# Attention scores from stacked high and low parts of queries and keys, in a two-layer network on one core

## The chip, the cores and the metric

The kernel runs on one core of one Trainium2 chip. The metric is the device time of one execution in microseconds (us). The core has TensorE for matrix products (PE in the profile, its weight loads PEld), VectorE (DVE), ScalarE (ACT), GpSimd (POOL) and the sync engine (SP), which here only issues transfers.

## The reference, cut to what matters

Two layers on 512 tokens of width 1024. Layer one mixes a convolution and a recurrence, layer two is attention in a sliding window of 128 with 16 query heads on 4 key heads of 64, and each is followed by a feed-forward part with a gate. The change is in the attention:

```python
q = partial_rope(rms_norm(q, q_norm_g), positions)
k = partial_rope(rms_norm(k, k_norm_g), positions)
...
s = jnp.einsum('bnqhgd,bnkhd->bnhgqk', q, kc).astype(jnp.float32) * (HEAD_DIM ** -0.5)
...
m = jnp.maximum(jnp.max(s, axis=-1, keepdims=True), sink)
pr = jnp.exp(s - m)
pr = pr / (jnp.sum(pr, axis=-1, keepdims=True) + jnp.exp(sink - m))
o = jnp.einsum('bnhgqk,bnkhd->bnqhgd', pr.astype(vc.dtype), vc)
```

Queries come in blocks of 128 tokens; each block sees its own 128 keys and the 128 before them.

## The kernel before, in words

Large products (`gemm`) run on parts: weights and activations are each split into a high part of type fp32r (a copy on ScalarE, line 150 or 183) and a low part (the difference on VectorE, line 151 or 184), and three fp32r products high·high, high·low and low·high are summed in PSUM (line 174). Weights come through SP's queue, 512 KB a transfer, into two buffers (`wraw`, line 139).

`attention` first makes the keys (two gemm blocks of 128 channels), normalises and rotates them (`rope`), and copies each key head by GpSimd's queue (line 867) into both halves of the rows of a tile `kd[m]`, so that either half of the rows can be the contraction. Then come the values (line 876, fp32r products with 256 moving columns), then eight `queries(j)`, each a gemm of 128 channels, two heads. In `rope` for queries, four small transfers on GpSimd's queue (line 835) swap the rotated rows into `zr`. The result lies in `qr[:, j, :]` in fp32, an even head in rows 0 to 63 and an odd one in rows 64 to 127. The queries' norm is not applied to `qr` but kept as a factor `rq` per token and head (lines 902 to 910).

`block(m, b)` treats key head `m` with its four query heads for token block `b`. It makes four fp32 products of 64 rows (line 931) into two PSUM banks `pscs`, one for even and one for odd heads; then, for each head, a VectorE instruction with mask, factor and running minimum (line 936) and an exponential on ScalarE (line 939, shown under the helper's line 101); sums and a reciprocal `dn`; four scalings by `dn` on VectorE (line 946); transposes on TensorE (950), copies on ScalarE (952), products with the values (957), and the split of the output (line 959). For `b = 0` there are 128 keys, otherwise 256. After all blocks the output projection follows, a gemm on `oh` and `ol`.

The calls are written in the order queries 0 and 1, then for each `m` four blocks with one more query ahead of blocks 0 and 2. A planner orders each engine's instructions when the program is built, by written order and by when it reckons that operands and buffers are ready, so that products of later queries stand between those of a block. On the chip each engine works in that fixed order. The scores' PSUM ring `c` has three banks, `a` and `b` have two, `d` has one; the temporary ring `t2` has five tiles.

Of the kernel before, what the change touches and what calls it, by code (L numbers as in the profile page):

```python
# [11 lines left out]
F32 = mybir.dt.float32  # L12
F32R = mybir.dt.float32r
I32 = mybir.dt.int32
AF = mybir.ActivationFunctionType
ALU = mybir.AluOpType
# [3 lines left out]
P = 128  # L20
T = 512
D = 1024
DC = D // P
NB = T // P
# [12 lines left out]
NKV = 4  # L37
HD = 64
# [7 lines left out]
T3 = 5  # L46
# [22 lines left out]
class Net:  # L69
# [734 lines left out]
    def attention(self):  # L804
        nc, tc, ap = self.nc, self.tc, self.ap
        V, S, G = nc.vector, nc.scalar, nc.gpsimd
# [8 lines left out]
        with ExitStack() as es:  # L815
            pool = lambda **k: es.enter_context(tc.tile_pool(**k))
            cst = pool(name="atb", bufs=1)
            tr = pool(name="att", bufs=3)
            t2 = lambda n: tr.tile([P, T], F32, tag="t2", name=n, bufs=T3)
# [3 lines left out]
                G.memset(z, 0.0)  # L823

            def rope(dst, z, j=None):
                t = tq("rp")
                if j is None:
                    pp = self.bank("d")
                    nc.tensor.matmul(pp, lhsT=self.perm, rhs=z, start=True, stop=True)
                    V.tensor_tensor(out=t, in0=pp, in1=sin, op=ALU.mult)  # L830
                else:
                    pp = zr[j % 2]
                    for o in (0, 8, HD, HD + 8):
                        i = o ^ 8
                        G.dma_start(pp[o : o + 8, :], z[i : i + 8, :])
                    V.tensor_tensor(out=t, in0=pp, in1=self.sgs, op=ALU.mult)
                V.tensor_tensor(out=dst, in0=z, in1=cos, op=ALU.mult)
                V.tensor_tensor(out=dst, in0=dst, in1=t, op=ALU.add)


            kd = [cst.tile([P, T], F32, name=f"kd{m}") for m in range(NKV)]
            pk = self.gemm(wq, 8, xh, xl)
            self.table("natural_log_exp_and_others")
            rstd = cst.tile([P, T], F32, name="rstd")
# [8 lines left out]
            for i in range(2):  # L853
                t = tq("zt")
                V.tensor_tensor(out=t, in0=pk[i], in1=rstd, op=ALU.mult)
                S.activation(out=t, in_=t, func=AF.Identity, bias=self.pc("attn_b_qkv", 8 + i))
                sq = tq("zs")
                S.activation(out=sq, in_=t, func=AF.Square)
                pss = self.bank("d")
                nc.tensor.matmul(pss, lhsT=self.bdv, rhs=sq, start=True, stop=True)  # L860
                rs = self.rsqrt_rows(tr, "t2", pss, 1e-6, "kr", ln=True)
                V.scalar_tensor_tensor(out=t, in0=t, scalar=self.pc("attn_k_norm_g"), in1=rs, op0=ALU.mult, op1=ALU.mult)
                kr = tq("kr")
                rope(kr, t)
                for e in range(2):
                    for o in range(2):
                        G.dma_start(kd[2 * i + e][o * HD : (o + 1) * HD, :], kr[e * HD : (e + 1) * HD, :])

            vt = cst.tile([P, NB, KD], F32, name="vt")
            pvs = [self.pmm() for _ in range(NB)]  # L870
# [10 lines left out]
                V.scalar_tensor_tensor(out=vt[:, b, :], in0=pvs[b][:, :KD], scalar=rt[:, b : b + 1], in1=self.bvr, op0=ALU.mult, op1=ALU.add)  # L881


            qr = cst.tile([P, 8, T], F32, name="qr")
            rq = cst.tile([P, NB, NH], F32, name="rq")

            def queries(j):
# [2 lines left out]
                V.tensor_tensor(out=t, in0=pq, in1=rstd, op=ALU.mult)  # L890
                sq = tq("zs")
                S.activation(out=sq, in_=t, func=AF.Square, bias=self.pc("attn_b_qkv", j))
                pss = self.bank("d")[:, 0:8].rearrange("p (b h) -> p b h", b=NB)

                for b in range(NB):
                    for i in range(0, P, 32):
                        nc.tensor.matmul(pss[i : i + 32, b, :], lhsT=sq[:, b * P + i : b * P + i + 32], rhs=self.bh, start=True, stop=True,
                                         tile_position=(0, i))
                S.activation(out=t, in_=t, func=AF.Identity, scale=self.pc("attn_q_norm_g"), bias=self.bg[:, j : j + 1])

                ms = tr.tile([P, NB, 2], F32, tag="ms", name="ms")
                V.tensor_scalar(out=ms, in0=pss, scalar1=1.0 / HD, scalar2=1e-6, op0=ALU.mult, op1=ALU.add)
                rope(qr[:, j, :], t, j)
                y0 = tr.tile([P, NB, 2], F32, tag="my", name="my")
                self.fn(out=y0, in_=ms, func=AF.Ln)
                self.fn(out=y0, in_=y0, func=AF.Exp, scale=-0.5)
                V.tensor_tensor(out=ms, in0=ms, in1=y0, op=ALU.mult)
                V.tensor_tensor(out=ms, in0=ms, in1=y0, op=ALU.mult)
                V.tensor_scalar(out=ms, in0=ms, scalar1=0.5 / 8, scalar2=-1.5 / 8, op0=ALU.mult, op1=ALU.add)
                V.tensor_tensor(out=rq[:, :, 2 * j : 2 * j + 2], in0=ms, in1=y0, op=ALU.mult)  # L910

            cst.tile([P, 112], F32, name="gap")
            oh = cst.tile([P, DC, T], F32R, name="oh")
            ol = cst.tile([P, DC, T], F32R, name="ol")

            def block(m, b):
# [8 lines left out]

                pscs = [self.bank("c").rearrange("p (g k) -> p g k", g=2) for _ in range(2)]
                for hp in range(2):
                    for e in range(2):
                        h = 4 * m + 2 * hp + e
                        hs = slice(e * HD, (e + 1) * HD)  # L930
                        nc.tensor.matmul(pscs[e][:, hp, :nk], lhsT=qr[hs, h // 2, bs], rhs=kd[m][hs, k0 : k0 + nk], start=True, stop=True)  # L931
                for hp in range(2):
                    for e in range(2):
                        i = 2 * hp + e
# [8 lines left out]
                V.tensor_tensor(out=dn, in0=dn, in1=nm, op=ALU.add)  # L943
                V.reciprocal(out=dn, in_=dn)
                for i in range(4):
                    V.tensor_scalar(out=pr_[:, i, :nk], in0=pr_[:, i, :nk], scalar1=dn[:, i : i + 1], scalar2=None, op0=ALU.mult)
                for kb in range(nkb):
                    pt = self.bank("b").rearrange("p (h q) -> p h q", h=4)
                    for i in range(4):
# [95 lines left out]
```

## Time and profile before

| | us |
|---|---|
| median of 3 runs (lowest to highest) | 1216.67 (1216.54 to 1217.11) |
| profiled execution | 1216.95 |
| its span, first to last instruction | 1215.2 |
| TensorE busy | 1194.8 |
| VectorE busy | 723.4 |
| ScalarE busy | 554.3 |
| GpSimd busy | 72.0 |

Times within the span count from its start. The attention's queries, scores and output lie between 695 and 815 us. An instruction's duration includes its latency, and instructions of one engine may overlap in the records; what one costs in a row of its kind is seen in the distance of their starts. An fp32 product stands in the trace as two records, an fp32r product as one.

### The profile page before, as it was taken

To read this page: it belongs to the slowest core of one execution; us is meant where nothing else is said; L and a number is where in the kernel's file an instruction comes from. 1 tells how busy PE (TensorE), PEld (TensorE's weight loads), DVE (VectorE), ACT (ScalarE), POOL (GpSimd) and SP (SyncE) were. 2 spreads that over 40 slices of the span, in tenths; PEclk is the share of its full clock that TensorE was granted. 3 is DMA by queue.
4 is the path that set the end of the run, shared out by engine and by line. 5 is a ranking of instruction groups with operands and counts; after the bars stand their busy time and mean duration, and the time that the engine had idled before them with its cause. 6 is when DMAs were issued, how large, how long until landed. Compare 5 with 4: busy or idle time off the path is not lost.

```text
span 1215.2 us, 16956 instructions
## 1 busy us (share of the span) xinstructions
PE 1194.8 (98%) x6419; PEld 940.5 (77%) x6419; DVE 723.4 (60%) x1366; ACT 554.3 (46%) x1035; POOL 72.0 (6%) x209
## 2 busy tenths in 40 slices
PE   6999999999999999999999999999999999999998
PEld 5777866568788888888888866668888888888886
DVE  6787866477766555553333778875555555553332
ACT  6878332374534444342222567764543343442221
POOL 4101031000100000000000031100000000000000
PEclk9999998999999999999999999999999999999999
DMA  6144291023322223233333231112222223233331
GB/s 191 37 130 113 96 221 38 2 88 103 97 92 104 94 97 104 87 104 96 96 96 95 87 95 57 41 36 90 101 90 101 103 89 104 88 103 112 113 113 61
DMA packets 65088, 114.43 MB, mean 94 GB/s; under 512 B 15680, under 2 KB 17936, under 8 KB 65008
## 3 DMA queue, kind: packets, MB, share of 16 engines
q1 hardware_dynamic: 60048, 102.25, 26.3%
q0 software_dynamic: 4816, 10.89, 3.5%
q8 instruction: 50, 0.82, 0.3%
q14 instruction: 30, 0.25, 0.1%
q10 hardware_dynamic: 144, 0.23, 0.1%
HBM read 105.40 MB, written 4.26 MB: 90 GB/s over the span
## 4 chain that ended last, share of the span: by engine, by line
PE 94%; DVE 2%; ACT 2%; DMA 1%; issue 1%; SPq 0%; DVEq 0%
PE mm L174 68%; PE bank L174 11%; PE mm L633 2%; PE bank L931 2%; PE bank L957 1%; PE bank L950 1%; PE ps L411 1%; PE ps L543 1%; DMA xT<-in_xT_dram 1%; PE ps L562 1%; PE ps L556 1%; PE ps L570 0%; PE bank L359 0%; PE ps L549 0%; PE ps L520 0%
## 5 line engine op out<-in xcount | busy, mean ns | idle before, releaser
L151 DVE TENSOR_TENSOR wlo<-wraw,whi 128x512 fp32r<-128x512 f32 x364 | 250.8, 690 | 348.0 <-ACT whi L150 347.4
L150 ACT CAST whi<-wraw 128x512 fp32r<-128x512 f32 x364 | 224.9, 619 | 421.3 <-PE mm L174 378.4
L174 PE MATMUL mm<-xgh,whi 128*128 128x512 f32 x896 | 350.9, 392 | 9.8 <-ACT whi L150 8.3
L174 PE MATMUL mm<-xgh,wlo 128*128 128x512 f32 x896 | 351.0, 392 | 0.2 <-DVE wlo L151 0.2
L174 PE MATMUL mm<-xgl,whi 128*128 128x512 f32 x896 | 350.5, 391 | 0.0
L174 PEld LDWEIGHTS mm<-xgh,whi 128*128 128x128 f32 x896 | 168.6, 188 | 47.0 <-ACT whi L150 10.1
L174 PEld LDWEIGHTS mm<-xgh,wlo 128*128 128x128 f32 x896 | 168.5, 188 | 38.7 <-issue 2.4
L174 PEld LDWEIGHTS mm<-xgl,whi 128*128 128x128 f32 x896 | 168.7, 188 | 35.8 <-issue 1.2
L174 PE MATMUL mm<-hh,whi 128*128 128x512 f32 x352 | 136.9, 389 | 0.0
L174 PE MATMUL mm<-hl,whi 128*128 128x512 f32 x352 | 136.9, 389 | 0.0
L174 PE MATMUL mm<-hh,wlo 128*128 128x512 f32 x352 | 136.9, 389 | 0.0
L174 PEld LDWEIGHTS mm<-hh,wlo 128*128 128x128 f32 x352 | 66.1, 188 | 13.8
L174 PEld LDWEIGHTS mm<-hh,whi 128*128 128x128 f32 x352 | 66.1, 188 | 13.8
L174 PEld LDWEIGHTS mm<-hl,whi 128*128 128x128 f32 x352 | 66.1, 188 | 13.5
L720 DVE SCALAR_TENSOR_TENSOR t<-gp,col,t 128x512 f32<-128x512 f32 x88 | 63.5, 745 | 0.0
L717 ACT ACTIVATE t<-gp,col 128x512 f32<-128x512 f32 x44 | 35.7, 816 | 35.3 <-DVE gp L715 34.7
L183 ACT CAST hh<-t 128x512 fp32r<-128x512 f32 x44 | 27.2, 622 | 36.8 <-DVE t L723 36.5
L715 DVE TENSOR_TENSOR gp<-mm,rstd 128x512 f32<-128x512 f32 x44 | 30.3, 692 | 17.3 <-PE mm L174 17.2
L723 DVE TENSOR_TENSOR t<-t,mm 128x512 f32<-128x512 f32 x44 | 30.1, 687 | 17.0 <-PE mm L174 17.0
L101 ACT ACTIVATE t<-t 128x512 f32<-128x512 f32 x44 | 27.7, 630 | 20.4 <-DVE t L720 20.3
L714 POOL MEMSET gp<- 128x2 f32 x44 | 4.5, 104 | 507.7 <-DVE t L720 451.0
L936 DVE CUSTOM_DVE_ANT_0 pr<-bank,mask,nsnk 128x256 f32<-128x256 f32 (+1 forms) x64 | 31.4, 503 | 1.9 <-PE bank L931 1.9
(328 smaller groups left out, 1433.6 us busy)
## 6 DMA issues: line engine op xcount, KB each, us to landing
wraw<-in_w_up_dram SPq DMA_DIRECT2D x88, 512.0 KB, 3.5
wraw<-in_w_down_dram SPq DMA_DIRECT2D x40, 512.0 KB, 3.5
wraw<-in_w_in_dram SPq DMA_DIRECT2D x22, 512.0 KB, 3.6
wraw<-in_w_qkv_dram SPq DMA_DIRECT2D x12, 512.0 KB, 3.5
wraw<-in_w_out_dram SPq DMA_DIRECT2D x8, 512.0 KB, 3.5
wraw<-in_w_o_dram SPq DMA_DIRECT2D x8, 512.0 KB, 3.5
st<-cpad POOLq DMA_DIRECT2D x24, 135.0 KB, 4.4
xT<-in_xT_dram SPq DMA_DIRECT2D x4, 512.0 KB, 8.2
```

The lines of the kernel that those rows point to most:

```text
L101: ins = self.nc.scalar.activation(**kw)
L150: nc.scalar.copy(hi, src)
L151: nc.vector.tensor_tensor(out=lo, in0=src, in1=hi.bitcast(F32), op=ALU.subtract)
L174: mm = lambda a, b, **kw: self.nc.tensor.matmul(ps, lhsT=a[:, i, k, :], rhs=b[:, kk, :], **kw)
L183: nc.scalar.copy(hi, src)
L633: nc.tensor.matmul(pc[b * 32 : b * 32 + 32, :], lhsT=dg[:, b, g, :], rhs=stk[b][:, 4 * g : 4 * g + T], start=g == 0, stop=g == 7, tile_pos ...
L715: V.tensor_tensor(out=gp[:, 2:], in0=pg[i], in1=rstd, op=ALU.mult)
L717: S.activation(out=t, in_=gp[:, 2:], func=AF.Identity, scale=self.pc("ffn_conv_w", (3 * l + 2) * FC + f), bias=self.pc("ffn_conv_b", l * F ...
L720: V.scalar_tensor_tensor(out=t, in0=gp[:, j : j + T], scalar=self.pc("ffn_conv_w", (3 * l + j) * FC + f), in1=t, op0=ALU.mult, op1=ALU.add)
L723: V.tensor_tensor(out=t, in0=t, in1=pu[i], op=ALU.mult)
L931: nc.tensor.matmul(pscs[e][:, hp, :nk], lhsT=qr[hs, h // 2, bs], rhs=kd[m][hs, k0 : k0 + nk], start=True, stop=True)
L936: V.tensor_tensor_reduce(out=pr_[:, i, :nk], in0=pscs[e][:, hp, :nk], in1=mask[:, 2 * P - nk :], op0=ALU.add, op1=ALU.min, scale=rq[:, b, ...
```

## The change

The keys are split into a high and a low part after the rotation (`ks`), and both parts are copied into `kd[m]`, now fp32r with two parts. The rotated queries, too, are split, and four transfers a query on SP's queue (`nc.sync`) lay the parts into `qs[m]`: for each pair of heads a tile of 128 rows that holds one head's high part in one half of the rows and its low part in the other. A score is then two products of 128 rows: the stacked query parts by the keys' high part (which stands in both halves) and by the keys' low part, summed in PSUM. They always take 256 keys. `qs` and `ks` share a ring of two tiles. The norm factors of the queries are worked out for two queries at once. Of the four scalings by `dn`, two go to GpSimd. The rotation's temporary moves from a ring of its own to `t2`, and two unused gaps in memory are resized.

```diff
             def rope(dst, z, j=None):
-                t = tq("rp")
+                t = t2("rp")
...
-            kd = [cst.tile([P, T], F32, name=f"kd{m}") for m in range(NKV)]
+            cst.tile([P, 56], F32, name="gap0")
+            kd = [cst.tile([P, 2, T], F32R, name=f"kd{m}") for m in range(NKV)]
+            pair = lambda n: tr.tile([P, 2, 2, T], F32R, tag="qs", name=n, bufs=2)
+            ks = pair("ks")
...
-                kr = tq("kr")
+                kr = t2("kr")
                 rope(kr, t)
+                self.split(ks[:, i, 0, :], ks[:, i, 1, :], kr)
                 for e in range(2):
                     for o in range(2):
-                        G.dma_start(kd[2 * i + e][o * HD : (o + 1) * HD, :], kr[e * HD : (e + 1) * HD, :])
+                        G.dma_start(kd[2 * i + e][o * HD : (o + 1) * HD].bitcast(F32), ks[e * HD : (e + 1) * HD, i].bitcast(F32))
...
-            qr = cst.tile([P, 8, T], F32, name="qr")
+            qs = {}
...
-                pss = self.bank("d")[:, 0:8].rearrange("p (b h) -> p b h", b=NB)
+                if j % 2 == 0:
+                    qs["ps"] = self.bank("d")[:, 0:16].rearrange("p (b i h) -> p b i h", b=NB, i=2)
+                pss = qs["ps"][:, :, j % 2]
...
-                ms = tr.tile([P, NB, 2], F32, tag="ms", name="ms")
-                V.tensor_scalar(out=ms, in0=pss, scalar1=1.0 / HD, scalar2=1e-6, op0=ALU.mult, op1=ALU.add)
-                rope(qr[:, j, :], t, j)
-                y0 = tr.tile([P, NB, 2], F32, tag="my", name="my")
...
+                qr = t2("qr")
+                rope(qr, t, j)
+
+                if j % 2 == 0:
+                    qs[j // 2] = pair("qs")
+                q = [tr.tile([P, T], F32R, tag="t2", name=n, bufs=T3) for n in ("qh", "ql")]
+                self.split(q[0], q[1], qr)
+                for e in range(2):
+                    for d in range(2):
+                        nc.sync.dma_start(qs[j // 2][d * HD : (d + 1) * HD, j % 2, e, :].bitcast(F32), q[d ^ e][e * HD : (e + 1) * HD, :].bitcast(F32))
+                if j % 2:
+
+                    ms = tr.tile([P, NB, 4], F32, tag="ms", name="ms")
+                    V.tensor_scalar(out=ms, in0=qs["ps"].rearrange("p b i h -> p b (i h)"), scalar1=1.0 / HD, scalar2=1e-6, op0=ALU.mult, op1=ALU.add)
+                    y0 = tr.tile([P, NB, 4], F32, tag="my", name="my")
...
+                    V.tensor_tensor(out=rq[:, :, 2 * j - 2 : 2 * j + 2], in0=ms, in1=y0, op=ALU.mult)
+
+            cst.tile([P, 56], F32, name="gap")
...
                 for hp in range(2):
-                    for e in range(2):
-                        h = 4 * m + 2 * hp + e
-                        hs = slice(e * HD, (e + 1) * HD)
-                        nc.tensor.matmul(pscs[e][:, hp, :nk], lhsT=qr[hs, h // 2, bs], rhs=kd[m][hs, k0 : k0 + nk], start=True, stop=True)
+                    for j in range(2):
+                        for e in range(2):
+                            nc.tensor.matmul(pscs[e][:, hp, :], lhsT=qs[m][:, hp, e, bs], rhs=kd[m][:, j, k0 : k0 + 2 * P], start=j == 0, stop=j == 1)
...
                 for i in range(4):
-                    V.tensor_scalar(out=pr_[:, i, :nk], in0=pr_[:, i, :nk], scalar1=dn[:, i : i + 1], scalar2=None, op0=ALU.mult)
+                    (G if i % 2 else V).tensor_scalar(out=pr_[:, i, :nk], in0=pr_[:, i, :nk], scalar1=dn[:, i : i + 1], scalar2=None, op0=ALU.mult)
```

## Rows read from the trace of the kernel before

**Rows 1.** The page: busy times, and the chain that ended last.

```profile
PE 1194.8 (98%) x6419; PEld 940.5 (77%) x6419; DVE 723.4 (60%) x1366; ACT 554.3 (46%) x1035; POOL 72.0 (6%) x209
...
PE 94%; DVE 2%; ACT 2%; DMA 1%; issue 1%; SPq 0%; DVEq 0%
```

**Rows 2.** Stretch: length, busy PE, PEld, DVE, ACT, POOL, clock, DMA.

```profile
715.00:815.00 100.00, 98.79 (x703) 62.64 (x702) 83.20 (x326) 74.09 (x227) 12.22 (x26) 1.00 0.14 42
```

**Rows 3.** Stretch, line 931 alone: length, PE, PEld, clock, DMA.

```profile
715.00:805.00 90.00, 26.55 (x128) 15.19 (x128) 1.00 0.15 47
```

**Rows 4.** Timeline of PE at the first blocks: start us, us, what.

```profile
719.18 0.92 PE L931 MATMUL bank<-kd,qr 64*128 64x128 f32 x6
...
720.83 0.40 PE L174 MATMUL bank<-xgl,whi 128*128 128x512 f32 x1
721.06 0.39 PE L174 MATMUL bank<-xgh,wlo 128*128 128x512 f32 x1
721.38 1.13 PE L931 MATMUL bank<-kd,qr 64*128 64x256 f32 x4
722.44 0.50 PE L174 MATMUL bank<-xgh,whi 128*128 128x512 f32 x1
722.77 0.40 PE L174 MATMUL bank<-xgl,whi 128*128 128x512 f32 x1
...
724.72 1.13 PE L931 MATMUL bank<-kd,qr 64*128 64x256 f32 x8
726.37 0.53 PE L950 MATMUL bank<-ident,pr 128*128 128x128 f32 x2 [0.52 <-DVE pr L946]
```

**Rows 5.** Waits of PEld, 715 to 805: us in total, times, longest.

```profile
PEld bank L931 <- issue: 4.1, 13, 0.4
```

**Rows 6.** Timeline of PE at the values' products.

```profile
681.46 0.28 PE L876 MATMUL mm<-whi,xgh 128*128 128x256 f32 x1
...
681.81 0.28 PE L876 MATMUL mm<-whi,xgh 128*128 128x256 f32 x1
```

**Rows 7.** ACT by shape, 715 to 815: count, busy, mean ns, idle before.

```profile
L150 ACT CAST whi<-wraw 128x512 fp32r<-128x512 f32 x14 | 8.7, 619 | 5.7 <-PE bank L174 5.7
```

**Rows 8.** Timeline of DVE, at the masks and at the first blocks.

```profile
312.42 0.88 DVE L219 TENSOR_TENSOR sq<-sq 128x512 f32<-128x512 f32 x1
313.22 0.88 DVE L151 TENSOR_TENSOR wlo<-wraw,whi 128x512 fp32r<-128x512 f32 x1
...
717.97 0.69 DVE L838 TENSOR_TENSOR qr<-qr,rp 128x512 f32<-128x512 f32 x1
...
725.44 0.68 DVE L838 TENSOR_TENSOR qr<-qr,rp 128x512 f32<-128x512 f32 x1
726.04 0.87 DVE L946 TENSOR_SCALAR pr<-pr,dn 128x128 f32<-128x128 f32 x4
...
728.82 0.87 DVE L946 TENSOR_SCALAR pr<-pr,dn 128x256 f32<-128x256 f32 x3
```

**Rows 9.** Timeline of POOL, at the masks and the keys' copies.

```profile
312.28 0.47 POOL L795 TENSOR_SCALAR_AFFINE_SELECT mask<-mask 128x256 f32<-128x256 f32 x1
...
313.01 0.55 POOL L796 TENSOR_SCALAR_AFFINE_SELECT mask<-mask 128x256 f32<-128x256 f32 x1
...
706.51 2.11 POOL L867 DMA_DIRECT2D kd<-kr  x4
```

**Rows 10.** DMA issues, 695 to 815: KB each, median us to landing.

```profile
wraw<-in_w_o_dram SPq DMA_DIRECT2D x5, 512.0 KB, 3.5
kd<-kr POOLq DMA_DIRECT2D x8, 128.0 KB, 2.8
```

**Rows 11.** DVE by shape, 715 to 815: count, busy, mean ns, idle before.

```profile
L946 DVE TENSOR_SCALAR pr<-pr,dn 128x256 f32<-128x256 f32 x48 | 13.9, 347 | 0.1
...
L184 DVE TENSOR_TENSOR ol<-bank,oh 128x256 fp32r<-128x256 f32 x15 | 6.4, 424 | 5.0 <-ACT oh L183 4.9
...
L946 DVE TENSOR_SCALAR pr<-pr,dn 128x128 f32<-128x128 f32 x16 | 3.6, 280 | 0.0
...
L908 DVE TENSOR_TENSOR ms<-ms,my 128x8 f32<-128x8 f32 x6 | 1.0, 160 | 0.0
```

**Rows 12.** Waits of SP's queue, 715 to 815: us in total, times, longest.

```profile
SPq L139 <- DVE wlo L151: 97.1, 7, 23.9
```

More of the change, by code (lines that the diff above doesn't have):

```diff
@@ L899, in queries @@
                 S.activation(out=t, in_=t, func=AF.Identity, scale=self.pc("attn_q_norm_g"), bias=self.bg[:, j : j + 1])
-                ms = tr.tile([P, NB, 2], F32, tag="ms", name="ms")
-                V.tensor_scalar(out=ms, in0=pss, scalar1=1.0 / HD, scalar2=1e-6, op0=ALU.mult, op1=ALU.add)
-                rope(qr[:, j, :], t, j)
-                y0 = tr.tile([P, NB, 2], F32, tag="my", name="my")
[L905 to L912, printed above, removed]
+                qr = t2("qr")
[11 more added lines that the diff above has]
+                    y0 = tr.tile([P, NB, 4], F32, tag="my", name="my")
+                    self.fn(out=y0, in_=ms, func=AF.Ln)
+                    self.fn(out=y0, in_=y0, func=AF.Exp, scale=-0.5)
+                    V.tensor_tensor(out=ms, in0=ms, in1=y0, op=ALU.mult)
+                    V.tensor_tensor(out=ms, in0=ms, in1=y0, op=ALU.mult)
+                    V.tensor_scalar(out=ms, in0=ms, scalar1=0.5 / 8, scalar2=-1.5 / 8, op0=ALU.mult, op1=ALU.add)
+                    V.tensor_tensor(out=rq[:, :, 2 * j - 2 : 2 * j + 2], in0=ms, in1=y0, op=ALU.mult)
+            cst.tile([P, 56], F32, name="gap")
             oh = cst.tile([P, DC, T], F32R, name="oh")
```

## The prediction

> **What bounds the kernel now.** I read the page's busy times first: TensorE is busy 98% of the span, every other engine 60% or less, and the chain that ended last is TensorE for 94% [rows 1]. That is an average, so I went to the stage of the change. The table by stretches shows 715 to 815 us, nearly the whole attention: TensorE busy 98.79 of 100 us at granted clock 1.00 (the 2.4 GHz level), VectorE 83.2, ScalarE 74.1, GpSimd 12.2 [rows 2]. The reader is to see two things: a microsecond of TensorE work that goes is a microsecond of time here, and VectorE and ScalarE have only some 17 and 26 us of slack behind it.
>
> **Scores, the work removed.** Restricted to the score line, the stretches show TensorE busy 26.55 us in 715 to 805 with 128 records [rows 3]. There are 64 products (16 blocks of 4 heads); each fp32 product is two records. In order of time, four records of 64x256 (two products) start at 721.38 and the next product follows at 722.44, so a product alone costs 0.53 us. At 724.72 eight records take the same 1.13 us, since there the even and odd heads, which lie on different 64 rows, run side by side [rows 4]. The mean (26.55/64 = 0.41) says that both happen. Before a group there is also a gap: the weight product at 721.06 starts 0.32 us before the score, where its neighbours follow in 0.23 [rows 4]. The waits show 13 such entries with no other cause [rows 5]; 13 x 0.09 = 1.2 us, which I count only at the favourable end, since entries from fp32 transposes stay.
>
> **Scores, the work added.** Each block now issues 2 head pairs x 2 key parts x 2 heads = 8 products, 128 rows by 128 columns with 256 moving columns, also in the first block of each group (128 columns before). 16 x 8 = 128. The trace has this very shape: the products of the values at line 876 are fp32r, 128*128, 128x256, and stand 0.12 us apart, each with its own weight load [rows 6]. 128 x 0.12 = 15.4 us. Net 15.4 - 26.55 = **-11.2 us**. Bounds: -12.4 with the entry gaps; -8.6 if 26 groups (twice the 13 entries, an estimate) still show 0.10 us each at their start, as weight products do after a score (0.33 from 722.44 to 722.77, with 0.23 as the pace) [rows 4].
>
> **Query parts and their way to the matmul.** Eight times: a ScalarE cast (0.62, by the weights' cast of the same 128x512) [rows 7], a VectorE subtraction and four transfers of 128 KB on SP's queue. VectorE's instructions overlap in the records: the 128x512 one at 725.44 lasts 0.68, and the next starts 0.60 later [rows 8], so I price by spacing. The second query's rotation ends at 718.66 [rows 8], and scores from it follow from 719.18 [rows 4]. Now they wait 0.62 + 0.69 + 0.53 (issue, as the keys' copies take it, four in 2.11 [rows 9]) + 2.8 (landing of these copies of the same 128 KB [rows 10]) = 4.6 us more. The cover is weight products of queries 2 and 3. It ends: in the trace TensorE already idles 0.52 us at 726.37, at the first transposes, with those products used up [rows 4]. Query 4's products (24 x 0.23 = 5.5 us) could be pulled ahead, if its weights are there. Bounds 0 and 4.6; I take **+2.5**, nearer the idle row than the cover, for the weights of query 4 were not used at 726.
>
> The keys' split (two casts, two subtractions) and copies of 256 KB (their landing between 2.8 for 128 KB and 3.5 for the 512 KB loads [rows 10]) move the keys about 2 us later. The last copies of before were issued by 708.62 [rows 9], 10.5 us ahead of the scores at 719.18: hidden. Without that cover it would be 2 us, within the same late start. On GpSimd's queue the copies stand in front of the first query's rotation transfers, but the second query decides.
>
> **VectorE and ScalarE.** Of the 64 scalings 32 leave VectorE: by spacing 0.26 (three in 0.87, one alone 0.35) for 24 wide ones and 0.20 for 8 narrow ones (four in 0.87, one alone 0.28) [rows 8, 11], 7.9 us. Added: 8 subtractions x 0.60 = 4.8. The normalisation of the queries runs for two queries at once: five small instructions of about 0.16 [rows 11], three pairs instead of six queries in the stretch, 15 x 0.16 = 2.4 us less. VectorE: 83.2 - 7.9 + 4.8 - 2.4 = 77.7 us. ScalarE: 74.1 + 8 x 0.62 - 6 x 0.2 = 77.9 (the two small activations, too, run once per pair; 0.2 is an estimate, from the 0.16 of VectorE's). The stretch shrinks to 88.8 us, so both stand at 88%, where they were at 83 and 74. VectorE waits 5.0 us in it for ScalarE at the output split alone [rows 11], and such waits grow with ScalarE's load. The matmul order is fixed at build time, so what comes late stops TensorE. Bounds 0 and 4 (VectorE's waits for ScalarE almost doubled); I take **+1.5**, near the lower end, as there is still work of other heads.
>
> **GpSimd.** The 32 scalings are not in the trace on this engine. Nearest is the masks' select of 128x256: 0.47 and 0.55 us [rows 9]. 32 x 0.55 = 17.6 beside 12.2: no bound. Four scalings took 1.1 us in line on VectorE; two on each side take about the same. VectorE pays, though: beside those two selects its 128x512 instructions took 0.88 instead of 0.69 [rows 8], 0.19 each. 32 x 0.19 = 6.1 us at worst, zero at best; the bounds of VectorE are 77.7 and 83.8.
>
> The Trainium skill, Advanced Engine Details and Errata, section VectorE Performance Modes, says that VectorE's second SBUF port is shared with GpSimd and that the two block each other; the trace agrees in sign (0.88 for 0.69). Full blocking would give the time of the second rival below instead of that of the first.
>
> **Sum**, against the profiled execution (1216.95, span 1215.2): -11.2 + 2.5 + 1.5 = -7.2, so 1209.75; the median of the runs lies 0.28 lower: **1209.5**. Its own range is 1206 to 1213.
>
> **Rivals.**
> VectorE becomes the bound. 83.8 us with the 0.19 above, 8.4 us of waits (half of its 16.8 idle us, 100 - 83.2, as the half that faster products don't shorten; the share is an estimate) and the start 4.6 late make 96.8 of the 100 us: about 1213.5. For it: both engines are near 88%; against: no instruction of that size on GpSimd has to meet one of VectorE's each time.
>
> The same port, harder, is the case on the other side. Place: each scaling on GpSimd. If VectorE stands still for all 0.55 us of it, 77.7 + 17.6 + 8.4 + 4.6 = 108.3, so 8 us slower: 1225. It decides from (100 - 77.7 - 8.4 - 4.6)/32 = 0.29 us per scaling; the row shows 0.19.
>
> SP's queue. The weight loads and the queries' copies now stand in one line, and SP spends 97.1 of 100 us there waiting until a weight buffer is free [rows 12]. A copy that waits for its pair's buffer (two buffers, and the keys' parts use one first) holds the next load; landing 3.5, cast 0.62 and subtraction 0.69 then come late, 4.8 us. Three pairs held: 14.4 - 11.2 = 3.2 slower plus the late start 2.5, about 1222. Against: weights are loaded two queries ahead. It decides from 8.7 us of held time.
>
> No stall at all: -12.4, 1204.3. For it: other heads' work is at hand; against: the idle row at 726.
>
> The new products cost no less than the old: at the 0.23 us of a 512-column product [rows 4] they would be 29 us, 2.9 slower: 1219.5. The rows at line 876 speak against it.
>
> **How the numbers follow.** Chances: forecast 0.60; no stall 0.10; VectorE bound 0.14; blocked port 0.05; SP's queue 0.09; no cheaper products 0.02. A measurement of this kernel tells 0.2% (2.4 us) from no change. Faster: 0.60 + 0.10 and most of the 0.14, 0.78; within: the rest of it and small holds, 0.08; slower 0.14. The range reaches from the case without a stall (1204.3) past 1213 to where a few holds begin, 1217.5.
>
> **What would show it.** Right: 128 score records, 0.12 us apart in a run, TensorE busy under 17 us on that line; first scores some 4 us later against the queries' products; GpSimd scalings of about 0.55. Wrong: TensorE idle more than 4 us in the stage, VectorE's 128x512 instructions well over 0.69 beside GpSimd, weight casts that wait for loads, or a granted clock under 1.00 after a long wait at the first block.

## The result, and the profile after

The changed kernel takes 1228.28 us (median of 4 runs, 1226.57 to 1230.6) where the kernel before took 1216.89 beside it: 1.0093 of its time [1.008, 1.0105], 11.4 us slower. The forecast was 1209.5, the range ended at 1217.5. The profiled execution took 1228.64 us, its span 1226.9.

The page of the changed kernel, first the busy times, then the chain that ended last (answers to [rows 1]):

```profile
PE 1194.2 (97%) x6419; PEld 946.1 (77%) x6419; DVE 724.2 (59%) x1324; ACT 557.3 (45%) x1037; POOL 104.6 (9%) x241
...
PE 91%; DVE 3%; ACT 3%; issue 1%; POOL 1%; DMA 1%; DVEq 0%; POOLq 0%
```

TensorE is recorded as busy for as long as before, 1194 us, although the change takes work from it. Where that comes from shows in the stretches of 15 us (columns as in [rows 2]):

```profile
715.00:730.00 15.00, 13.72 (x120) 10.38 (x119) 9.66 (x18) 7.10 (x13) 4.00 (x8) 1.00 0.56 150
...
760.00:775.00 15.00, 12.66 (x60) 7.86 (x58) 11.57 (x38) 8.32 (x27) 6.23 (x8) 0.77 0.43 110
...
790.00:805.00 15.00, 12.47 (x67) 8.22 (x65) 11.30 (x39) 9.16 (x28) 7.58 (x9) 0.89 0.41 107
...
820.00:835.00 15.00, 13.96 (x65) 9.82 (x66) 6.39 (x13) 7.59 (x13) 2.22 (x5) 0.89 0.10 34
```

From 690 to 835 us (one stretch of 25 us and eight of 15) TensorE stands idle for 14.4 us, where it stood 1.5 us before. The granted clock falls below 1.00 in three of them: 15 x (0.23 + 0.11 + 0.11) = 6.75 us of full speed that are not granted; before it was 1.00 throughout. Busy time hides this second loss, because products at the lower clock count as busy for longer. These two sums, idle and clock loss, are worked out in the same way for every run below. They also give an estimate of TensorE's work: the span grew by 11.7 us, idle and clock loss by 12.9 and 6.75, so some 8 us of work are gone, where the prediction had 11.2.

TensorE's timeline shows one such place:

```profile
759.90 0.63 PE L946 MATMUL bank<-kd,qs 128*128 128x256 f32 x4
760.50 0.65 PE L972 MATMUL bank<-pT,vt 128*64 128x256 f32 x4
762.78 0.30 PE L965 MATMUL bank<-ident,pr 128*128 128x128 f32 x1 [1.63 <-DVE pr L961]
763.40 0.55 PE L965 MATMUL bank<-ident,pr 128*128 128x128 f32 x3 [0.32 <-POOL pr L961]
764.31 1.11 PE L965 MATMUL bank<-ident,pr 128*128 128x128 f32 x4 [0.36 <-POOL pr L961]
765.45 1.12 PE L972 MATMUL bank<-pT,vt 128*64 128x256 f32 x4
```

And VectorE in the same microseconds:

```profile
759.61 0.68 DVE L184 TENSOR_TENSOR ql<-qr,qh 128x512 fp32r<-128x512 f32 x1
760.59 0.16 DVE L958 TENSOR_TENSOR dn<-dn,nm 128x4 f32<-128x4 f32 x1 [0.29 <-ACT nm L101]
760.67 0.54 DVE L951 CUSTOM_DVE_ANT_0 pr<-bank,mask,nsnk 128x256 f32<-128x256 f32 x1
...
761.61 0.42 DVE L184 TENSOR_TENSOR ol<-bank,oh 128x256 fp32r<-128x256 f32 x1 [0.39 <-ACT oh L183]
761.95 0.17 DVE L959 RECIPROCAL dn<-dn 128x4 f32<-128x4 f32 x1
...
762.29 0.75 DVE L961 TENSOR_SCALAR pr<-pr,dn 128x256 f32<-128x256 f32 x2
```

No weight product stands in TensorE's order between a block's products with the values and the next transposes. TensorE waits for scalings that stand on VectorE behind a query's split, another block's mask and the output's split. After this wait the clock goes to the lower of its two levels. In stretches of 2 us:

```profile
761.00:763.00 2.00, 0.37 (x3) 0.14 (x1) 1.58 (x9) 1.95 (x10) 0.68 (x1) 1.00 0.83 216
763.00:765.00 2.00, 1.33 (x7) 1.01 (x7) 2.00 (x11) 0.45 (x2) 2.00 (x3) 0.71 0.01 2
765.00:767.00 2.00, 1.97 (x7) 0.60 (x6) 1.86 (x4) 1.95 (x6) 1.57 (x2) 0.50 0.00 0
767.00:769.00 2.00, 2.00 (x9) 1.23 (x9) 0.41 (x2) 0.84 (x3) 0.00 (x0) 0.50 0.00 0
769.00:771.00 2.00, 2.00 (x11) 1.83 (x9) 2.00 (x7) 0.69 (x3) 0.00 (x0) 0.58 0.34 80
771.00:773.00 2.00, 2.00 (x13) 1.16 (x13) 1.55 (x4) 1.44 (x5) 0.00 (x0) 1.00 0.89 194
```

What that costs can be read above: four products with the values take 0.65 us at 760.50 and the same four 1.12 at 765.45.

The first scores come 11 us later than the 715.5 us of before, when 113 of the 192 weight products of the queries have been worked off instead of 73. By the first transposes it is 144 instead of 96:

```profile
726.38 0.47 PE L946 MATMUL bank<-kd,qs 128*128 128x256 f32 x2 [0.16 <-DMA zr<-zt]
```

The new products have the pace that was forecast: eleven in a row take 1.58 us, the last one's own 0.28 taken off 0.13 apart, and seven take 1.08:

```profile
744.60 1.58 PE L946 MATMUL bank<-kd,qs 128*128 128x256 f32 x11
...
752.03 1.08 PE L946 MATMUL bank<-kd,qs 128*128 128x256 f32 x7
```

GpSimd's scalings do not take what was forecast. By line (count: shortest/median/longest ns), then VectorE's by shape (as in [rows 11]), and the waits of TensorE from 715 to 835:

```profile
L961 POOL TENSOR_SCALAR pr<-pr,dn x32: 607/947/1687, 737.5 to 821.7; 128x256 f32<-128x256 f32 x24, 128x128 f32<-128x128 f32 x8
L961 DVE TENSOR_SCALAR pr<-pr,dn x32: 274/438/580, 737.9 to 820.5; 128x256 f32<-128x256 f32 x24, 128x128 f32<-128x128 f32 x8
```

```profile
L961 DVE TENSOR_SCALAR pr<-pr,dn 128x256 f32<-128x256 f32 x24 | 10.4, 470 | 0.1
...
L961 DVE TENSOR_SCALAR pr<-pr,dn 128x128 f32<-128x128 f32 x8 | 2.2, 315 | 0.0
```

```profile
PE bank L965 <- POOL pr L961: 5.5, 10, 1.1
PE bank L972 <- ACT pT L967: 2.7, 6, 0.7
PE bank L965 <- DVE pr L961: 2.1, 3, 1.6
```

### The profile page after: what moved, and what is told of

Same layout as the page of the kernel before. It is cut to its first block, busy times and chain, and to the rows that moved or that the text cites. A ratio compares the mean times of both kernels' runs of the same rounds, so it can differ in the third digit from the quotient of the medians.

```text
span 1226.9 us, 17089 instructions
## 1 busy us (share of the span) xinstructions
PE 1194.2 (97%) x6419; PEld 946.1 (77%) x6419; DVE 724.2 (59%) x1324; ACT 557.3 (45%) x1037; POOL 104.6 (9%) x241
## 4 chain that ended last, share of the span: by engine, by line
PE 91%; DVE 3%; ACT 3%; issue 1%; POOL 1%; DMA 1%; DVEq 0%; POOLq 0%
PE mm L174 68%; PE bank L174 9%; PE mm L633 2%; PE bank L972 1%; PE bank L965 1%; PE bank L946 1%; PE ps L411 1%; POOL pr L961 1%; PE ps L543 1%; PE ps L562 1%; PE ps L556 1%; ACT pT L967 1%; PE ps L570 0%; DMA xT<-in_xT_dram 0%; PE bank L359 0%
## 5 line engine op out<-in xcount | busy, mean ns | idle before, releaser
L715 DVE TENSOR_TENSOR gp<-mm,rstd 128x512 f32<-128x512 f32 x44 | 30.3, 692 | 17.3 <-PE mm L174 17.2
L961 POOL TENSOR_SCALAR pr<-pr,dn 128x256 f32<-128x256 f32 (+1 forms) x32 | 32.1, 1012 | 48.6 <-DVE dn L959 22.1
```

Source lines behind the costliest of these rows:

```text
L715: V.tensor_tensor(out=gp[:, 2:], in0=pg[i], in1=rstd, op=ALU.mult)
L961: (G if i % 2 else V).tensor_scalar(out=pr_[:, i, :nk], in0=pr_[:, i, :nk], scalar1=dn[:, i : i + 1], scalar2=None, op0=ALU.mult)
```

## The experiments

All were timed beside the kernel before. Ratios are to it, on the same chip; idle and clock loss are TensorE's from 690 to 835 us in the profiled execution, and belong to that one execution (k2's took 1229.0 us against its median of 1223.4). Differences in us in the text are those of two medians, against the kernel before with its median of the same chip (1216.8 to 1217.3). Unless its order is held, as below, each variant got an order of its own from the planner, so its difference is that of the edit and of the order together.

| | median us | ratio [95%] | idle us | clock loss us |
|---|---|---|---|---|
| before | 1216.9 | 1 | 1.5 | 0 |
| the change | 1228.3 | 1.0093 [1.008, 1.0105] | 14.4 | 6.8 |
| e1_all_vector | 1223.7 | 1.0052 [1.004, 1.0064] | 11.9 | 1.7 |
| e2_before_half_gpsimd | 1223.7 | 1.0057 [1.0045, 1.0069] | 6.2 | 0 |
| e3_one_gpsimd | 1222.9 | 1.0044 [1.0031, 1.0058] | 11.2 | 1.7 |
| f1_three_products | 1235.4 | 1.0121 [1.0087, 1.0154] | 7.1 | 8.6 |
| f2_swap_on_sync | 1226.0 | 1.006 [1.0042, 1.0078] | 11.8 | 5.1 |
| f3_before_copies | 1219.9 | 1.0019 [1.0009, 1.003] | 0.8 | 0 |
| g1_high_only | 1224.8 | 1.0065 [1.0051, 1.0079] | 8.9 | 13.7 |
| g2_split_only | 1219.6 | 1.0025 [1.0015, 1.0035] | 1.3 | 0 |
| g3_no_query_split | 1220.0 | 1.0019 [1.001, 1.0027] | 8.9 | 3.5 |
| h1_high_only_old_order | 1213.9 | 0.9973 [0.9964, 0.9983] | 6.1 | 6.9 |
| h2_e1_old_order | 1239.5 | 1.0175 [1.0158, 1.0192] | 22.0 | 15.3 |
| h3_f2_old_order | 1235.8 | 1.0155 [1.0141, 1.0168] | 21.7 | 8.6 |
| i1_e1_order_of_old_products | 1229.3 | 1.0095 [1.008, 1.0111] | 13.5 | 1.7 |
| i2_f2_order_of_old_products | 1224.5 | 1.0059 [1.0046, 1.0072] | 13.4 | 3.5 |
| i3_after_order_of_old_products | 1224.4 | 1.0061 [1.0044, 1.0077] | 13.4 | 0 |
| i4_all_but_products | 1234.1 | 1.0144 [1.0124, 1.0163] | 9.7 | 6.9 |
| k1_before_new_order | 1237.3 | 1.0161 [1.0147, 1.0175] | 8.2 | 8.4 |
| k2_each_norm | 1223.4 | 1.0043 [1.003, 1.0057] | 11.7 | 5.1 |

### GpSimd's scalings: e1, e2, e3

```diff
 e1, from the change:
-                    (G if i % 2 else V).tensor_scalar(out=pr_[:, i, :nk], ...)
+                    V.tensor_scalar(out=pr_[:, i, :nk], ...)
 e2, the kernel before with
+                    (G if i % 2 else V).tensor_scalar(out=pr_[:, i, :nk], ...)
 e3, from the change, with one of the four on GpSimd
```

> The changed kernel with all four scalings of a block on VectorE again; everything else of the change stays. Theory A (the two scalings on GpSimd, about 1.0 us each, make the transposes late, TensorE idles and its clock falls): the time falls from 1228 to 1207 to 1213, faster than the kernel before, the granted clock is back at 0.996 and TensorE waits for no scaling longer than 0.5 us. Rival B (the late first scores, at 726 instead of 715, which the query parts and their copies cause, are the loss): the first scores stay at 726 and the time stays at 1222 or more.

> The kernel before with one edit: two of the four scalings of a block on GpSimd. Theory A: slower than before by 8 to 20 us, the scalings on GpSimd last about 1.0 us as in the changed kernel, and TensorE waits for them. Rival B: within 3 us of the kernel before, since its blocks start in time and other heads' work covers the scalings.

> The changed kernel with one of the four scalings of a block on GpSimd (the last) and three on VectorE. Theory A: between the changed kernel and the one with all on VectorE, near the latter if what counts is two GpSimd scalings in line (2 us against 0.7), since one of 1.0 us stands beside three of VectorE: 1208 to 1216. Rival B: at or above 1222, as with two.

Without GpSimd the change is 4.6 us faster (1223.7), but still 6.5 above the kernel before: rival B's value, though B gave a late start as the reason. On the kernel before, GpSimd's half costs 6.5 us, between what the two theories said. One scaling of four (1222.9) costs nothing that can be told from none. In e2 the scalings take as long as in the change, and TensorE waits for them (by line, then who waited for it: us, times):

```profile
L946 POOL TENSOR_SCALAR pr<-pr,dn x32: 594/946/1444, 727.6 to 818.4; 128x256 f32<-128x256 f32 x24, 128x128 f32<-128x128 f32 x8
...
  PE bank L950: 4.2, 10
```

So GpSimd's scalings are not the whole loss: 6.5 of 11.4 us stay without them. The rest of the runs ask what makes these 6.5 us.

### The late start and the copies: f1, f2, f3

```diff
 f1, from e1: no copies, parts in place, three products of 64 rows (low by low left out)
+                self.split(qs[j // 2][:, j % 2, 0, :], qs[j // 2][:, j % 2, 1, :], qr)
...
+                    for n, (i, j) in enumerate(((0, 0), (1, 0), (0, 1))):
...
+                            nc.tensor.matmul(pscs[e][:, hp, :], lhsT=qs[m][hs, hp, i, bs], rhs=kd[m][hs, j, k0 : k0 + 2 * P], start=n == 0, stop=n == 2)
 f2, from e1: the rotation's transfers of the first two queries on SP's queue
-                        G.dma_start(pp[o : o + 8, :], z[i : i + 8, :])
+                        (nc.sync if j < 2 else G).dma_start(pp[o : o + 8, :], z[i : i + 8, :])
 f3, from the kernel before: four copies of each fp32 query on SP's queue into a ring of two
+                        nc.sync.dma_start(qs[j // 2][e * HD : (e + 1) * HD, j % 2, d, :], qr[e * HD : (e + 1) * HD, :])
```

> The changed kernel with all scalings on VectorE, and without the copies of the query parts: the two parts of the queries stay in place (even head in rows 0 to 63, odd head in rows 64 to 127), and a score is three products of 64 rows, high by high, low by high, high by low; low by low is left out. Theory B (late first scores are the loss that all scalings on VectorE leaves): the first scores come about 4 us earlier than at 727.6 and the time falls by 3 to 8 us from 1223.7, to 1216 to 1221. Theory C (VectorE and ScalarE are the bound of the blocks, whatever the start): it stays within 2 us of 1223.7.

> The changed kernel with all scalings on VectorE, and one more edit: the small transfers that swap the rotated rows of queries 0 and 1 go by SP's queue, so that they no longer stand behind the keys' copies of 256 KB on GpSimd's queue. In the order that was built the first score then stands behind 82 weight products of queries instead of 113 (73 in the kernel before). Theory B: the first scores move from 727.6 to about 720, and the time falls by 4 to 8 us from 1223.7. Theory C: the first scores move and the time stays within 2 us.

> The kernel before with one edit: each rotated query, in fp32 and not split, is copied by four transfers of 128 KB on SP's queue into a ring of two tiles, as the changed kernel does with the parts, and the scores read the copy (two of the four copies are not read). Theory B: the first scores come 3 to 5 us late, and the time rises by 2 to 6 us. Theory C: within 1.5 us of the kernel before, as the TensorE work is the same and weight products cover the wait.

The late start does not explain the loss. f2 starts its scores at 718.4 us, 8 us earlier than e1, and gains nothing (1226.0, nearest to theory C); TensorE idles later instead (12.55 and 12.02 of 15 us busy from 745 to 775). f2 also points to where most of the late start comes from: in the change the last of the first query's rotation transfers goes out at 711.0 us on GpSimd's queue, behind four copies of keys that start at 709.0. f3 has the queries' copies; its scores start 6 us later in the trace, but its profiled execution was already 3 us late ahead of the attention, so 3 us are the copies' (83 weight products instead of 73). TensorE idles no more than before, and f3 costs 2.6 us, as theory B said. f1 has no copies at all and its six runs take 1227 to 1239 us, outside both of its theories; with 192 products of 64 rows it is another kernel in its scores, too.

### Each part by itself: g1, g2, g3

```diff
 g1, the kernel before with fp32r tiles, one product of 64 rows as before
-            qr = cst.tile([P, 8, T], F32, name="qr")
+            qr = cst.tile([P, 8, T], F32R, name="qr")
...
-            kd = [cst.tile([P, T], F32, name=f"kd{m}") for m in range(NKV)]
+            kd = [cst.tile([P, T], F32R, name=f"kd{m}") for m in range(NKV)]
 g2, the kernel before with
+                q = [tr.tile([P, T], F32R, tag="t2", name=n, bufs=T3) for n in ("qh", "ql")]
+                self.split(q[0], q[1], qr[:, j, :])
 g3, from e1; the rotation's result is fp32r and the copies read it
-                self.split(q[0], q[1], qr)
```

> The kernel before, with queries and keys rounded to fp32r and one product of 64 rows a head in place of the fp32 one: the low parts are left out, nothing is split, copied or moved. It takes TensorE's work away and adds nothing. If the stage is bound by TensorE, as the prediction says, 64 products at about a third of the 27 us that 192 such records took in the variant with three products are 9 us, 17 less than 26.55: 1199 to 1203. If the chain of VectorE and ScalarE (83 and 74 of 100 us busy) binds as soon as TensorE has less to do, most of it comes back as idle TensorE: 1208 to 1214. If what TensorE saves is wholly paid back, as with all scalings on VectorE: 1216 or more.

> The kernel before, with the queries' split added (8 casts on ScalarE, 8 subtractions on VectorE, into tiles that nothing reads); scores, copies, keys and scalings as before. If the split's place in the two in-order queues delays the scalings and exponentials that TensorE waits for, this alone is 4 to 8 us slower: 1221 to 1225. If the split is hidden, as the prediction's slack of 17 and 26 us says: 1217 to 1219.

> The variant with all scalings on VectorE, without the queries' split: the rotation writes fp32r, and the four copies lay this one part into both places (the low parts are left out; copies, products, keys and normalisation stay). If the split is what eats the saving: 1211 to 1216, TensorE idle in the stage under 6 us (11.6 with the split). If it is the copies, their landing or the built order: 1221 to 1224, as with the split.

The split costs 2.5 us where it is added (g2) and gives 3.8 where it is taken out (g3); both lie between their two expectations. g1 was the surprise: cheaper products, with nothing else edited, make the kernel 7.7 us slower, the last of its three alternatives. Its clock loss is 13.7 us, most of it in one stretch. TensorE there in slices of 2 us (busy, clock, DMA share, GB/s):

```profile
788.00:790.00 2.00, 2.00 (x13) 1.00 0.05 8
790.00:792.00 2.00, 0.84 (x4) 1.00 0.00 0
792.00:794.00 2.00, 0.91 (x4) 0.81 0.00 0
794.00:796.00 2.00, 2.00 (x9) 0.50 0.00 0
...
816.00:818.00 2.00, 2.00 (x10) 0.71 0.18 28
```

But, the clock aside, a product that takes less cannot make an engine late that works in the same order. The order was not the same. In g1's trace the first scores stand behind 73 weight products, as before (h1's expectation below has 96, which is f1's number), but by the first transposes 108 are worked off and not 96, and from there on the blocks' scores and transposes come in another sequence. The edit of one kind of product changed the order on TensorE, VectorE and ScalarE.

### The order by itself: h1, k1

In h1, k1, i1, i2 and i3 every instruction of the attention on an engine gets an edge to the one ahead of it in an order read from another built program; in h2 and h3 this is done on TensorE alone. The edges set the order of issue and add no semaphore.

```diff
+        seq = [mine[r] for r in rank]
+        for a, b in zip(seq, seq[1:]):
+            net.tc.add_manual_dep(b, a.name, mybir.DependencyInfo(mybir.DependencyClass.NoSync, mybir.DependencyReason.DATA), reason="order")
```

> The variant with one fp32r product of 64 rows a head (high parts alone), with the instructions of the attention held in the order of the kernel before on every engine, by order edges without semaphores; nothing else changed. If the new order that the planner makes out of cheaper products is what costs time (its first scores stand behind 96 weight products instead of 73, with fewer of them left between a block's transposes), the time falls below the kernel before: 1200 to 1211, granted clock 1.00 in the stage. If the chain of VectorE and ScalarE gives the time back whatever the order: 1215 to 1218; if TensorE's idle time also lowers the clock: 1220 to 1226, as without the held order.

> The kernel before, its fp32 products and all its other instructions unchanged, with every engine's order in the attention held to the order that the planner made for the variant with one fp32r product of high parts. If an order is what loses the time there, it loses it with the old products too: 1222 to 1230. If the order is harmless and the idle TensorE of the cheaper products (with its lowered clock) is the loss: 1216 to 1219.

| | products of before | cheaper products |
|---|---|---|
| order of before | 1216.9 | 1213.9 (h1) |
| order planned for the cheaper products | 1237.3 (k1) | 1224.8 (g1) |

The order alone costs 10.9 us with the cheaper products and 20 with the old ones. The cheaper products gain in either order, 2.9 and 12.5 us. That the idle TensorE of the cheaper products is g1's loss, k1's second alternative, is ruled out: with the old products in that order the loss is larger, above the range of k1's first alternative, too. h1 lies between its first two.

h1 also shows how little TensorE's time is worth in the order of before. Its score line alone, then its whole stretch from 715 to 815 us (beside [rows 2, 3]):

```profile
715.00:815.00 100.00, 14.19 (x64) 8.16 (x64) 0.93 0.15 45
...
715.00:815.00 100.00, 94.14 (x645) 59.33 (x644) 83.14 (x327) 73.37 (x227) 12.12 (x26) 0.93 0.15 45
```

The products take 26.55 - 14.19 = 12.4 us less, and idle and clock loss grow by 4.6 and 6.9, which leaves 0.9; the profiled execution gains 1.5 and the median 2.9. The clock does not explain it all: h1's three fastest executions (1212.0 to 1212.3 us) had a mean granted clock of 0.996, as the kernel before has (0.993 to 0.999, mostly 0.997), and they gain some 4.6 us. VectorE and ScalarE do as much as before in the same 100 us (83.14 and 73.37). They carry the blocks from scores to output, and TensorE now waits for them; the longest entry among its waits from 700 to 850 us is for scalings on VectorE:

```profile
PE bank L950 <- DVE pr L946: 3.8, 4, 1.4
```

### Other orders for the change: h2, h3, i1, i2, i3

h2 and h3 hold TensorE to the order of the kernel before, in e1 and f2. i1, i2 and i3 hold all engines of e1, f2 and the changed kernel to the order that the planner makes for the same program with the old kind of product in it.

> The variant with all scalings on VectorE, with TensorE's instructions of the attention held in the order of the kernel before (each old pair of scores replaced by its four new products); the other engines are planned. The first scores then stand behind 73 weight products and TensorE has to stand still until the query parts have landed, some 8 us by the variant's first scores at 727. If the planner's order is the cause of the loss: -10 for the products and +8 for the start, 1213 to 1219. If the chain is the cause: 1222 to 1228.

> The same held order in the variant whose rotation transfers of the first two queries go on SP's queue, where the parts land at 718: about 3 us behind the scores of the kernel before. If the planner's order is the cause: -10 and +3, 1207 to 1212, under the kernel before. If the chain of VectorE and ScalarE is the cause, it stays at 1222 to 1227 as with the planned order (1225.95).

> The variant with all scalings on VectorE (1223.7), all its transfers, splits and new products kept, but every engine's order in the attention held to the one that the planner makes when the scores are the old fp32 products (each pair of them replaced by its four new ones). If the order planned from cheaper products costs here what it cost the variant with high parts alone (10.6 us): 1211 to 1216, under the kernel before. If copies, split and the chain of VectorE and ScalarE cost it whatever the order: 1221 to 1226.

> The same in the variant with the first two queries' rotation transfers on SP's queue, whose planned order stands at 1226. If the order is the cause: 1209 to 1215, and it would be the fastest of all that keep the low parts. If the chain is: 1223 to 1228.

> The changed kernel itself, two of four scalings on GpSimd, with the order held in the same way. By the order as the cause: 4 to 6 us above the variant without GpSimd (the price of GpSimd's scalings), 1216 to 1221, and well below the changed kernel's 1228.3. By the chain as the cause: 1226 to 1230.

None beats the kernel before. h2 and h3 lie above all their expectations, i1 too; i2 is where its second alternative has it, and i3 between its two. In h3 the old order asks for each pair's scores before its parts have landed (the waits of TensorE, 700 to 850):

```profile
PE bank L946 <- DMA qs<-ql: 14.6, 4, 5.6
```

Here the copies do cost, at every pair of queries and not only at the first. The planner's order for e1 avoids most of this wait by using up weight products ahead (144 by the first transposes), and then lacks them later. Of the other three, i1 is 5.6 us slower than e1, i2 cannot be told from f2 (1.5 us), i3 is 3.9 faster than the change. So i3, with GpSimd, stands 4.9 us below i1, without: the 4.6 us between the change and e1 include a difference of orders of that size, and are no clean price for GpSimd.

### All but the products, and the norm factors: i4, k2

```diff
 i4, from e1: fp32 products of 64 rows, of the high parts alone
+                        nc.tensor.matmul(pscs[e][:, hp, :nk], lhsT=qs[m][hs, hp, e, bs].bitcast(F32), rhs=kd[m][hs, 0, k0 : k0 + nk].bitcast(F32), start=True, stop=True)
 k2, from e1: per query, as before
+                V.tensor_scalar(out=ms, in0=pss, scalar1=1.0 / HD, scalar2=1e-6, op0=ALU.mult, op1=ALU.add)
...
+                V.tensor_tensor(out=rq[:, :, 2 * j : 2 * j + 2], in0=ms, in1=y0, op=ALU.mult)
```

> All of the change but two parts: scores from the old kind of product (fp32, 64 rows, high part by high part alone; the low parts are split and copied but not used), all scalings on VectorE. By the sum of the two parts measured alone (copies 2.3, split 3.0): 1221 to 1224, so that the new products, which save 10 us of TensorE's time, are worth nothing under the planned order. If the new products do bring their 10 us and something else costs 16: 1230 or more.

> The variant with all scalings on VectorE, with the norm factors of the queries worked out for each query as before instead of for two at once. If the pair's common factors, which come after the second query, are a part of the 17 us that all but the products cost: 1216 to 1221. If not, 15 small VectorE instructions of 0.16 us are added (2.4 us in the stage): 1223 to 1227.

i4 is 17.3 us slower than the kernel before, as its second alternative has it, and e1, with the new products, is 10.4 us faster than i4. This is not the price of the products. i4 is the program whose order i1 is held to: in the two traces all engines work in the same order, groups of scores counted as one. So e1, i1 and i4 make a second table:

| all scalings on VectorE | old products, high parts | new products |
|---|---|---|
| order planned for the old products | 1234.1 (i4) | 1229.3 (i1) |
| order planned for the new products | not run | 1223.7 (e1) |

In the same order the new products gain 4.8 us, and the order that the planner made for them gains another 5.6. Here, unlike in g1, the order for the cheaper products is the better one. The score line alone in i4, then in e1 (columns as in [rows 3]):

```profile
715.00:835.00 120.00, 28.96 (x128) 17.01 (x128) 0.94 0.27 75
...
715.00:835.00 120.00, 23.49 (x128) 17.71 (x128) 0.99 0.30 82
```

The two ways of working out the norm factors (k2 and e1) differ by 0.3 us, within what can be told, as k2's second alternative has it.

## Why the prediction was wrong

**The step that failed: "a microsecond of TensorE work that goes is a microsecond of time here".** h1 takes 12.4 us of work off the score line, keeps the order of before and leaves VectorE and ScalarE with what they had (83.14 and 73.37 us). It gains 2.9 us, and some 4.6 where the clock is not lower than before. The rest comes back as idle TensorE and as a lower clock. In the change itself TensorE stands idle for 12.9 us more than before and loses 6.75 us to the clock; the sum had +4.0 for everything that is not work, and nothing for the clock.

**Products, -11.2: the pace right, the size not.** The new products stand 0.13 us apart in a row, as forecast. But the sum sets them at this pace against the busy time of the old ones, which holds the latency at the end of each short group (a new product alone lasts 0.28 us, in a row it costs 0.13). Measured alike, the score line has 26.55 us before [rows 3] and 23.49 in e1, 3.1 us less; the sign "under 17 us" failed for the same reason. For what the whole span gets back there are estimates: e1's profiled execution has 12.0 us more of idle and clock loss than the kernel before and is 5.8 us longer in its span, so some 6 us of work are gone, and i4 against i1, in one order, gives 5.9 in the same way. In the medians these two differ by 4.8 us.

**Query parts, +2.5 (0 to 4.6): a term of the right size, for the wrong thing.** The copies cost 2.6 us in f3. But the first scores came 11 us later and not 4.6. The prediction saw that the keys' copies stand in front of the first query's rotation transfers and set this aside ("the second query decides"); with these transfers on SP's queue, in f2 and its own order, the scores come 8 us earlier. The planner filled the 11 us with 40 weight products (113 - 73; at the 0.23 us of [rows 4] 9.2 us of work) that it then lacked in the later blocks. An earlier start alone gained nothing in f2.

**VectorE and ScalarE, +1.5 (0 to 4): the loads right, the slack not.** The split costs 2.5 us (g2), within the bounds. VectorE's sum was about right (77.7 forecast, 78.87 from 715 to 815, a stretch that holds somewhat different work). What was wrong is to read 17 and 26 us of slack from such sums: h1, with VectorE's work unchanged, shows that TensorE can use little of it.

**GpSimd, 0.55 us each, "no bound": too small by 0.4 us.** The median is 0.95. The mask's select was a poor neighbour for a scaling with a factor for each row. VectorE's own scalings in the change take 470 and 315 ns in the mean where [rows 11] had 347 and 280; the prediction put the cost on its 128x512 instructions. (The Trainium skill, Advanced Engine Details and Errata, section VectorE Performance Modes, says that GpSimd and those instructions of VectorE that use both of its SBUF ports block each other, as one port is shared; the trace agrees in sign, by 0.12 us for a wide scaling, and no run shows whether a scaling is such an instruction. No VectorE scaling of the change takes longer than 0.58 us, in e2 one takes 1.02.) TensorE waits 5.5 us for GpSimd's scalings. With all on VectorE the change is 4.6 us faster, in another order.

**What the sum left out: the order.** It adds parts to the order of before. The prediction said itself that the order is fixed at build time, but not that the program would get another one. The parts that it priced at +4.0 (copies, split, late start) cost 2.6 (copies, with a part of the late start) and 2.5 (split), each in its own order, and 17.3 together with the rest of the change (i4). Some 12 us of this belong to no part that was measured by itself. An order alone made 10.9 and 20 us in h1, g1 and k1, so it can be of this size. That the 12 us are the order is not shown: no order tried for the changed program was a good one, and against the order for the old products the planner's own was 5.6 us better in e1, 3.9 worse in the change and not to be told apart in f2. The keys' split and their larger copies, and the ring that the rotation's temporaries share, were not undone alone, so what they cost stays open.

Of the rivals, the blocked port came nearest in time (1225), by luck, for a reason that is a minor part. "VectorE becomes the bound" came nearest to the mechanism, though not by VectorE's load: TensorE meets the chain of VectorE and ScalarE, block by block, when its fillers are gone. SP's queue held copies for a query's split, but TensorE's waits in the stage name no weight part. Two signs listed as "wrong" appeared: more than 4 us of idle TensorE (14.4), and a clock under 1.00 after a long wait (0.77), though not at the first block. Three listed as "right" did not: scalings of about 0.55 on GpSimd, under 17 us on the score line, and first scores some 4 us later.

## What to carry to other kernels

In a stage where three engines are 74 to 99% busy and a planner writes the order, an edit is priced in the order that it will have: build both, hold one order in the other program, and the part that is the order shows itself. It can be a loss (g1) or a gain (e1 against i1). TensorE at 99% says that it always has something to do, not that less of it would end sooner: in the order of before, 12.4 us less gained 2.9, and in the order planned for the cheaper products the same exchange gained 12.5. Work that moves to a slower engine is counted by when the next engine needs it, not by that engine's share of busy time.

## What the hardware showed

A wait of TensorE is followed by a lower clock only sometimes. In the change, 0.37 us of work in 761 to 763 was followed by 0.71, 0.50, 0.50 and 0.58 in the next four slices. In g1 the low level lasted until 817, with TensorE recorded busy for most of that time. In e1 TensorE did nothing from 765 to 767 and the clock stayed at 1.00:

```profile
765.00:767.00 2.00, 0.00 (x0) 0.00 (x0) 2.00 (x10) 1.21 (x4) 0.00 (x0) 1.00 0.19 44
767.00:769.00 2.00, 1.70 (x12) 1.19 (x14) 2.00 (x9) 1.16 (x4) 0.00 (x0) 1.00 0.88 202
```

What decides between the two is not settled by these runs. Executions of one kernel differ in it, too: h1's twelve lie between 1212.0 us at a mean clock of 0.996 and 1216.4 at 0.991.
